# A hybrid decoder layer on one core: norm rows by a store and a broadcast load, and eleven norms' sums by VectorE's 32x32 transposes

## The chip, the cores and the metric

The kernel runs on one core of a Trainium2 chip, as one launch. The metric is the device time of the execution in microseconds, the median of three runs. A core has five engines with a queue each: TensorE (PE, with its weight loads as PEld), VectorE (DVE), ScalarE (ACT), GpSimd (POOL) and SyncE (SP, which here only issues DMAs).

## The reference

One decoder layer on a residual stream of 1024 tokens by 1024 features, float32. Four blocks follow one another; each norms its input, computes, norms its output, and adds it to the stream:

```python
def rmsnorm(x, g):
    y = x32 * lax.rsqrt(jnp.mean(x32 * x32, axis=-1, keepdims=True) + EPS)
    return y * g

h = x
h = h + 0.5 * rmsnorm(swiglu(rmsnorm(h, ffn1_pre_g), ...), ffn1_post_g)
h = h + rmsnorm(hybrid_mixer(rmsnorm(h, mix_pre_g), ...), mix_post_g)
h = h + rmsnorm(memory_cross_attention(rmsnorm(h, xa_pre_g), rmsnorm(mem, mem_g), ...), xa_post_g)
h = h + 0.5 * rmsnorm(swiglu(rmsnorm(h, ffn2_pre_g), ...), ffn2_post_g)
```

The mixer has stick-breaking attention (its output normed with `attn_norm_g`) beside a Mamba-2 SSD scan (its output gated and normed in two groups of 512 features with `ssd_norm_g`), and one output projection for both. So there are some twenty norms for 1024 tokens each, and one for the 256 memory tokens.

## The kernel before, in words

Activations stand with features on the 128 partitions and tokens along the free axis, in two halves (`hh` 0 and 1) of H = 512 tokens and KT = 8 tiles of 128 features: `F[hh][d]` is a block's output, `h[hh][d]` the stream in DRAM, `XH`/`XL` the next block's input as a high and a low part. A float32 matmul is made of three products of such parts (`mm3`), each 128x128 by 128x512.

A norm needs, for each token, a sum of squares over all features, so over the partitions. ScalarE squares the tiles and VectorE adds them into one tile of 128x512 (`sumsq`, line 361). `rms_cols` then multiplies each block of 128 tokens as the stationary operand with a column of 1/1024 (or 1/512): four products of one column give the mean squares of 512 tokens as a column `c` (128 tokens on the partitions, four blocks), followed by a root on ScalarE (L341) and a reciprocal on VectorE (L342). To scale tiles whose tokens lie along the free axis, `rms_rows` turns the column into a row on all 128 partitions: it multiplies each block of `c`, broadcast to 128 columns, with the identity, and ScalarE copies the result from PSUM into `r` (L355). Both use the PSUM tile `ms`, of which there is one; attention's and the scan's transposes use it too.

`post` is the norm of a block's output with the sum into the stream and the norm for the next block: `cols` and `rows` for `r` (`rpost`), `apply` scales and adds (L407, L411), `low` makes the low part (L423), `presum` sums squares for the next norm, whose column and row are `c2` (`cpre`) and `r2_` (`rpre`). `pre` is the same for a norm alone. Where a projection's result leaves PSUM it is multiplied with `rpre` (`evac`), or with `rn` in the mixer's output projection (`norm_row`, `mix_sum`). The columns alone are used as scales in the scores of both attentions.

The order on TensorE is written out: each matmul is tied behind the one before it. `self.clock` adds up modelled TensorE time in ns; a function on `self.later` runs when the clock passes its time, so that its matmuls stand at that place, and `pinned(t)` puts a group there without tying what follows in the program. A planner orders the other queues by its own estimates and by what each instruction waits for; `kp` keeps an instruction of a `later` function in program order. SP's queue is in order too: a DMA that waits for a buffer or for data holds all behind it. Weights come over SP (`wtile`, L182 and L185; `wstream` loads one tile ahead, three buffers).

At the start of attention, `inproj(0)` projects Q, K and V of the first pair of heads. V is transposed in 32x32 blocks on VectorE, stored (L1727), and loaded back with four DMAs that put the blocks in place (L1731); `vtr` splits it. `kevac` writes K's parts to the tiles `k` with four DMAs for each half (`rows`, L1700).

Of the kernel before, what the change touches and what calls it, by code (L numbers as in the profile page):

```python
# [18 lines left out]
P = 128  # L19
S = 1024  # L20
H = 512
# [4 lines left out]
MIXED = 6  # L26
# [21 lines left out]
class Kern:  # L48
# [272 lines left out]

    def rms_cols(self, groups, c, ones=None, r2=None):


        nc = self.nc
        ps = self.t(self.msp, [P, H], F32, "ms", bufs=1)
        nb = 0
        for g, accs in enumerate(groups):
            w = ones[g] if isinstance(ones, list) else self.ones if ones is None else ones
            for b in range(accs[0].shape[1] // P):  # L330
                for i, acc in enumerate(accs):
                    self.mm(
                        ps[:, nb : nb + 1], acc[:, b * P : (b + 1) * P], w, i == 0, i == len(accs) - 1
                    )
                nb += 1
        if r2 is not None:
            self.kp(nc.vector.tensor_tensor(out=c, in0=ps[:, 0:nb], in1=r2, op=ALU.mult))
            self.kp(nc.vector.tensor_tensor(out=c, in0=c, in1=r2, op=ALU.mult))
            self.kp(nc.scalar.activation(c, c, AF.Sqrt, bias=self.eps))
        else:  # L340
            self.kp(nc.scalar.activation(c, ps[:, 0:nb], AF.Sqrt, bias=self.eps))  # L341
        self.kp(nc.vector.reciprocal(c, c))  # L342
        if r2 is not None:
            self.kp(nc.vector.tensor_tensor(out=c, in0=c, in1=r2, op=ALU.mult))

    def rms_rows(self, c, r, behind=None):
# [38 lines left out]

    def post(self, hh, gname, r2, gnext=None, out=None, step=None, spread=True, pins=(23000, 28000), accs=None, at=None, tail=None, hold=False, late=None):

# [8 lines left out]
        r = self.t(self.fp, [P, H], F32, "rpost", bufs=1)  # L396

        def cols():
            self.rms_cols([accs], c, r2=r2)

        def rows():
            self.rms_rows(c, r)

# [79 lines left out]

    def pre(self, hh, accs, t1, t2):
        c = self.t(self.rp, [P, 4], F32, f"cpre{hh}", bufs=2)
        r = self.t(self.rp, [P, H], F32, f"rpre{hh}", bufs=1)
        with self.pinned(t1):
            self.rms_cols([accs], c)
        with self.pinned(t2):
            self.rms_rows(c[:, :], r)  # L490
        self.R[hh], self.C[hh] = r, c
# [487 lines left out]
    def down1(self, sp, wdn, act_d, xs_d, gpost, gnext):  # L979
# [15 lines left out]
        def finish(m, i):  # L995
            if m == 3:
                self.run_later(float("inf"))
                for d in range(4):
                    at(5000 + 4000 * d, squares, 0, d, "acc0")
                self.resid(0, 3500, 16000)  # L1000
            elif m == 4:
                self.run_later(float("inf"))
                for d in range(4, 8):
                    squares(0, d, "acc0")
                self.XH[0] = [self.t(self.xp, [P, H], F32R, f"xh0{d}") for d in range(KT)]
                self.post(0, gpost, self.C[0], gnext, step=2600, accs=accs[:], tail=(20500, 24000), late=38000)
# [9 lines left out]
        self.XH[1] = [self.t(self.xp, [P, H], F32R, f"xh1{d}") for d in range(KT)]  # L1016
        self.post(1, gpost, self.C[1], gnext, step=2000, accs=accs[:], at=(6500, 9000, 10000), tail=(7500, 10500))

# [231 lines left out]
    def ssd(self, close):  # L1250

        nc, ap = self.nc, self.ap
        with self.tc.tile_pool(name=self.nm("ssa"), bufs=1, reuse_waits="tile") as ep, \
# [271 lines left out]
            def group_norm(gr):  # L1525
                c = self.norm_c[gr] = self.t(self.rp, [P, 8], F32, f"cy{gr}")
                self.rms_cols([[y] for y in yacc], c, ones=self.ones512)

# [19 lines left out]
            def keys(n0, n1):  # L1548

                mh, ml, acc, rm = env["mem"]  # L1550
                if n0 == 0:
                    self.mem_c = self.t(self.rp, [P, 2], F32, "cmem")
                    self.rms_cols([[acc]], self.mem_c)
# [93 lines left out]
    def attention(self):  # L1647
        nc, ap = self.nc, self.ap
        with self.pools("at", ["o", "a"], ["w"]) as (op, sp, wsp, pp):
# [52 lines left out]
            def inproj(p):  # L1702
# [12 lines left out]
                def steps(hh, t, before):  # L1715
# [13 lines left out]
                    rows = o.rearrange("(c e) (j q d) -> q e j c d", c=4, q=4, d=32)  # L1729
                    for q in range(4):  # L1730
                        nc.sync.dma_start(  # L1731
                            out=v[32 * q : 32 * q + 32, :].rearrange("e (j c d) -> e j c d", j=4, c=4), in_=rows[q]
                        )
                    return v

# [43 lines left out]
                for n in range(6):  # L1779
# [25 lines left out]
            def mix_row(i):  # L1805
                self.mix_r.append(self.t(self.rp, [P, H], F32, f"rpre{i}", bufs=1))
                return self.rms_rows(self.norm_c[i][:, 0:4], self.mix_r[i], tr_tile)

# [108 lines left out]
            def memory_values(mh, ml):  # L1917

                rm = self.t(self.tp, [P, H], F32, "sq1")[:, 0:MEM]
                self.rms_rows(self.mem_c[:, :], rm)  # L1920
                yield
# [30 lines left out]
            def beside():  # L1952
                late.append(mix_row(1))
                self.first = self.mix_first(ready.pop())
                for n in range(4 * MIXED):
                    if n < 2:
                        for k in ((5, 6), (7,))[n]:
                            mix_split(k)
                    if n == 2:
                        late.pop()()  # L1960
                    if 4 <= n < 11:
# [8 lines left out]
            wo = [self.wsrc("out", 8 * part + d) for n in range(2) for part in (1, 0) for d in range(8)]  # L1970
            self.Wo, self.mix_r, ready, late = self.wstream(wo[0:MIXED]), [], [], []
            for p in range(7):
# [37 lines left out]
    def mix_out(self):  # L2010
# [3 lines left out]
        with self.pools("mo", ["r", "a"], ["b"]) as (rp, sp, sp2, dnp):  # L2014
# [53 lines left out]
            for n, (hh, part) in enumerate(passes):  # L2068
# [3 lines left out]
                def norms(t):  # L2072
                    c = self.norm_c[2] = self.t(self.rp, [P, 4], F32, "ca", bufs=2)
                    with self.pinned(self.clock + t):
                        self.rms_cols([asum[-1:]], c)
                    R[2] = norm_row(2, 0, t + 4000)
# [32 lines left out]
                if n == 1:  # L2109
                    self.run_later(float("inf"))  # L2110
                    self.post(0, "mix_post_g", None, "xa_pre_g", step=5000, spread=False, accs=ends[0], at=(6000, 11500, 14000), tail=(18000, 0))
                    self.resid(1, 5000, 17000)
                if n == 3:
                    self.flush(0)
                    self.post(1, "mix_post_g", None, "xa_pre_g", step=3000, spread=False, accs=ends[1], at=(6000, 10500, 13000), hold=True)


    def xattn(self):
# [3 lines left out]
        with self.pools("xf", ["a", "b", "w"], []) as (sp, sp2, wsp, pp):  # L2122
# [107 lines left out]
            for s in range(8):  # L2230
# [3 lines left out]
                if s == 4:  # L2234
# [5 lines left out]
                    self.run_later(float("inf"))  # L2240
                    self.post(0, "xa_post_g", None, "ffn2_pre_g", step=5000, at=(8500, 16000, 19000))
                if s == 3:
# [46 lines left out]
    def run(self):  # L2289
        nc, tc, ap = self.nc, self.tc, self.ap  # L2290
        with tc.tile_pool(name="const", bufs=1) as cp, tc.tile_pool(name="state", bufs=1, reuse_waits="tile") as xp, \
# [5 lines left out]
            self.place(tp, 64)  # L2297
            self.place(cp, 448)
            self.params = self.t(cp, [P, NPAR], F32, "params")
# [16 lines left out]
            def consts():  # L2316
                cst = self.t(self.fp, [P, 2, P], F32, "rpost")
                nc.sync.dma_start(out=cst, in_=ap["consts"])
                nc.scalar.copy(self.ident, cst[:, 0, :])
                nc.scalar.copy(self.tri, cst[:, 1, :])  # L2320
                for g in (self.par(n, 0, 8) for n in ("ffn1_post_g", "ffn2_post_g")):
# [152 lines left out]
```

## Time and profile before

| | us |
|---|---|
| median of 3 runs (2585.55 to 2587.47) | 2585.72 |
| the profiled execution | 2583.27 |
| its span, first to last instruction | 2581.5 |
| TensorE busy with matmuls | 2564.0 (99%) |
| TensorE's weight loads | 2141.0 (83%) |
| VectorE busy | 2000.7 (78%) |
| ScalarE busy | 1289.0 (50%) |
| GpSimd busy | 576.5 (22%) |

Matmuls overlap in their pipeline, so durations of single ones (some 390 ns for 512 columns) add up to more than the span; what one occupies is the distance from its start to the start of the next. In rows of a timeline the first number is the start, the second the time until the end of the group; "L139" is the line of `mm`, through which nearly every matmul goes, "L142" that of a transpose; "ms<-small,acc" reads: into tile `ms`, from the tiles `small` (the column of ones) and `acc`. "x8" is the number of records; a float32 product has two. A wait in square brackets is the engine's idle time before the instruction, and who ended it. "SPq" is SP's issue of a DMA.

### The profile page before, as it was taken

To read this page: it belongs to the slowest core of one execution; us is meant where nothing else is said; L and a number is where in the kernel's file an instruction comes from. 1 tells how busy PE (TensorE), PEld (TensorE's weight loads), DVE (VectorE), ACT (ScalarE), POOL (GpSimd) and SP (SyncE) were. 2 spreads that over 40 slices of the span, in tenths; PEclk is the share of its full clock that TensorE was granted. 3 is DMA by queue.
4 is the path that set the end of the run, shared out by engine and by line. 5 is a ranking of instruction groups with operands and counts; after the bars stand their busy time and mean duration, and the time that the engine had idled before them with its cause. 6 is when DMAs were issued, how large, how long until landed. Compare 5 with 4: busy or idle time off the path is not lost. (4 is left out here: it accounts for less than half of the span.)

```text
span 2581.5 us, 36855 instructions
## 1 busy us (share of the span) xinstructions
PE 2564.0 (99%) x12786; PEld 2141.0 (83%) x12786; DVE 2000.7 (78%) x3074; ACT 1289.0 (50%) x2302; POOL 576.5 (22%) x674
## 2 busy tenths in 40 slices
PE   9999999999999999999999999999999999999999
PEld 7888888888787778888888898888888888888887
DVE  7988997779689884787787876876656887777777
ACT  7434444555356663555555654455554433334453
POOL 2555553001000001111111110111012655541000
PEclk9999999999999999999999999999999999999999
DMA  6458988655665516666666655547658443327654
GB/s 240 163 180 293 308 290 305 220 185 166 232 205 197 184 72 212 186 177 160 176 171 152 206 167 202 197 155 260 202 185 304 150 162 111 110 82 237 192 175 147
DMA packets 251628, 498.24 MB, mean 193 GB/s; under 512 B 60592, under 2 KB 69168, under 8 KB 251440
## 3 DMA queue, kind: packets, MB, share of 16 engines
q1 hardware_dynamic: 204176, 387.31, 46.4%
q0 software_dynamic: 23360, 65.03, 8.6%
q10 hardware_dynamic: 23904, 43.53, 4.6%
q8 instruction: 101, 1.65, 0.3%
q14 instruction: 87, 0.71, 0.1%
HBM read 331.65 MB, written 143.13 MB: 184 GB/s over the span
## 5 line engine op out<-in xcount | busy, mean ns | idle before, releaser
L139 PE MATMUL mm<-xh,whi 128*128 128x512 f32 x1312 | 516.7, 403 | 1.1 <-DVE ft L668 0.5
L139 PE MATMUL mm<-xh,wlo 128*128 128x512 f32 x1280 | 491.7, 392 | 0.0
L139 PE MATMUL mm<-xl,whi 128*128 128x512 f32 (+1 forms) x1248 | 485.7, 389 | 0.3 <-DVE xl L277 0.3
L139 PEld LDWEIGHTS mm<-xh,wlo 128*128 128x128 f32 x1280 | 240.6, 188 | 52.4 <-DVE wlo L270 0.5
L139 PEld LDWEIGHTS mm<-xh,whi 128*128 128x128 f32 x1312 | 247.0, 188 | 43.1 <-issue 3.9
L139 PEld LDWEIGHTS mm<-xl,whi 128*128 128x128 f32 x1248 | 235.6, 189 | 33.4 <-DVE xl L277 0.8
L1829 DVE TENSOR_TENSOR_SCAN nb<-nb,begin 128x128 f32<-128x128 f32 (+7 forms) x128 | 172.1, 1347 | 32.3 <-ACT nb L1825 31.9
L1825 ACT ACTIVATE nb<-z,scale 128x128 f32<-128x128 f32 (+2 forms) x192 | 109.5, 580 | 89.5 <-PE z L139 88.6
L270 DVE TENSOR_TENSOR wlo<-wraw,whi 128x1024 fp32r<-128x1024 f32 x61 | 74.6, 1223 | 51.3 <-ACT whi L268 50.9
L268 ACT CAST whi<-wraw 128x1024 fp32r<-128x1024 f32 (+1 forms) x77 | 73.9, 959 | 70.4 <-PE mm L139 43.5
L1846 POOL DMA_DIRECT2D mix<-sq x64 | 53.0, 828 | 248.7 <-DVE sq L1844 181.5
L669 ACT ACTIVATE ft<-ft 128x512 f32<-128x512 f32 x88 | 55.5, 632 | 95.5 <-DVE ft L668 94.9
L139 PE MATMUL dn<-xh,wlo 128*128 128x512 f32 x296 | 101.2, 390 | 0.0
L772 POOL TENSOR_TENSOR wc<-raw,wraw 128x512 f32<-128x512 f32 x55 | 80.7, 1467 | 56.4 <-DVE wlo L270 23.4
L268 ACT CAST ath<-tr 128x512 fp32r<-128x512 f32 (+1 forms) x106 | 57.3, 540 | 66.9 <-PE tr L142 61.9
L772 POOL TENSOR_TENSOR wc<-wraw,raw 128x512 f32<-128x512 f32 x56 | 78.9, 1409 | 52.5 <-DVE whi L270 16.5
L871 POOL TENSOR_TENSOR ft<-ft,e 128x512 f32<-128x512 f32 x37 | 59.7, 1614 | 126.3 <-DVE e L867 51.1
L270 DVE TENSOR_TENSOR atl<-tr,ath 128x512 fp32r<-128x512 f32 (+1 forms) x106 | 66.1, 625 | 28.0 <-ACT ath L268 26.9
L139 PE MATMUL mm<-ath,v 128*128 128x256 f32 x320 | 87.8, 297 | 0.0
L139 PE MATMUL dn<-xh,blk 128*128 128x512 f32 x264 | 85.2, 389 | 0.0
L268 ACT CAST wlo<-wc 128x512 fp32r<-128x512 f32 x79 | 49.1, 621 | 69.2 <-PE dn L139 25.4
L139 PE MATMUL mm<-atl,v 128*128 128x256 f32 x320 | 83.1, 282 | 0.0
(601 smaller groups left out, 6795.2 us busy)
## 6 DMA issues: line engine op xcount, KB each, us to landing
whi<-dwhi SPq DMA_DIRECT2D x82, 512.0 KB, 4.1
wlo<-dwlo SPq DMA_DIRECT2D x82, 512.0 KB, 5.4
wraw<-in_w_gu SPq DMA_DIRECT2D x43, 512.0 KB, 4.0
dwhi<-bh SPq DMA_DIRECT2D x78, 256.0 KB, 4.2
dwlo<-bl SPq DMA_DIRECT2D x78, 256.0 KB, 4.2
raw<-in_w_gu SPq DMA_DIRECT2D x37, 512.0 KB, 4.1
wraw<-xs SPq DMA_DIRECT2D x56, 256.0 KB, 2.9
xs<-ft ACTq DMA_DIRECT2D x54, 256.0 KB, 3.0
```

The lines of the kernel that those rows point to most:

```text
L139: self._pe(self.nc.tensor.matmul(out, lhsT, rhs, start=start, stop=stop, skip_group_check=self.more), cost)
L268: self.kp(self.nc.scalar.copy(hi, src))
L270: self.nc.vector.tensor_tensor(out=lo, in0=src, in1=hi.bitcast(F32), op=ALU.subtract)
L669: nc.scalar.activation(t, t, AF.Silu)
L772: inst = (nc.vector if early else nc.gpsimd).tensor_tensor(out=t, in0=a, in1=b, op=op)
L871: nc.gpsimd.tensor_tensor(out=t1, in0=t1, in1=e, op=ALU.mult)
L1825: nc.scalar.activation(nb[:, s0:s1], z[:, 0:n], AF.Sigmoid, scale=sc[:, i : i + 1])
L1829: nc.vector.tensor_tensor_scan(out=nb[:, 0:Wd][:, ::-1], data0=nb[:, 0:Wd][:, ::-1], data1=begin[:, S - Wd : S][:, ::-1], initial=0.0, op0 ...
L1846: nc.gpsimd.dma_start(out=self.mix_d[p][a * 64 : a * 64 + 64, csl], in_=o, accum_op=ALU.add)
```

## The change

`rms_cols` keeps the column in DRAM as well: it stores `c`, in pieces of four bytes, as rows of 128 tokens (`kept`). `row` loads such rows, broadcast over the 128 partitions, into `r`; it takes the place of `rms_rows` in `post` (except the second half after FFN1, `pe=True`), in the norms of the mixer's output projection, in the memory's norm, and in attention for the gated group norms. The input's norms and the last one before FFN2 (`pre`) stay on TensorE.

`turned` takes the place of `rms_cols` for eleven sets of 512 tokens: both gated group norms (two sets each), the next-block norms of both halves after FFN1, the mixer's output norms of both halves, the next-block norm of the mixer's first half, and both norms of the first half after cross-attention. VectorE transposes the tile of squares in 32x32 blocks in place and sums runs of 32; that leaves, for each token, four partial sums in the four quarters of the partitions. One product with `quads`, four 32x32 identities one above the other, adds the quarters: 32 partitions by 16 columns. Root, reciprocal and a store of four-byte pieces follow; where the column is needed too, it is loaded back from there.

Beside that, in `inproj(0)` the loads of the second half of V are issued behind K's, and `vtr(1, ...)` follows; the gated norm's row for the first pass is loaded at step 8 rather than made at steps 10 and 12; and the second half's `apply` in the mixer starts at 14000 rather than 13000.

```diff
-    def rms_cols(self, groups, c, ones=None, r2=None):
+    def rms_cols(self, groups, c, ones=None, r2=None, keep=True):
 ...
+        if keep:
+            kept = self.tc.dram_tile([nb, P], F32, name=self.nm("norm"))
+            nc.sync.dma_start(out=kept.rearrange("b p -> p b"), in_=c)
+            return kept
+
+    def turned(self, accs, ms, wait=0, c=None):
+        nc = self.nc
+        kept = self.tc.dram_tile([4 * len(accs), P], F32, name=self.nm("norm"))
+        ps = self.t(self.msp, [P, H], F32, "ms", bufs=1)
+        parts = []
+        for acc in accs:
+            self.turns = 1 - self.turns
+            parts.append(self.part[self.turns])
+            self.kp(nc.vector.transpose(acc, acc))
+            self.kp(nc.vector.tensor_reduce(out=parts[-1][0], in_=acc.rearrange("p (j k) -> p j k", k=32), op=ALU.add, ...))
+        with self.pinned(self.clock + wait):
+            for n, (part, _) in enumerate(parts):
+                self.mm(ps[0:32, 16 * n : 16 * n + 16], self.quads, part, True, True)
+        for n, (_, x) in enumerate(parts):
+            self.kp(nc.scalar.activation(x, ps[0:32, 16 * n : 16 * n + 16], AF.Sqrt, bias=self.eps[0:32], scale=ms))
+            self.kp(nc.vector.reciprocal(x, x))
+            nc.sync.dma_start(out=kept[4 * n : 4 * n + 4].rearrange("b (q i) -> i (b q)", i=32), in_=x)
+        if c is not None:
+            nc.sync.dma_start(out=c, in_=kept.rearrange("b p -> p b"))
+        return kept
+
+    def row(self, kept, r):
+        self.nc.sync.dma_start(out=r, in_=kept.rearrange("b p -> (b p)").partition_broadcast(P))
 ...
         def cols():
-            self.rms_cols([accs], c, r2=r2)
+            if turn[0]:
+                kept.append(self.turned(accs, 1.0 / D_MODEL, 2000))
+            else:
+                kept.append(self.rms_cols([accs], c, r2=r2, keep=not pe))
         def rows():
-            self.rms_rows(c, r)
+            if pe:
+                self.rms_rows(c, r)
+            else:
+                self.row(kept[0], r)
 ...
-            self.held = [lambda: self.rms_cols([accs2], c2)]
+            self.held = [lambda: kept.append(self.turned(accs2, 1.0 / D_MODEL, 2000, c2) if turn[1]
+                                             else self.rms_cols([accs2], c2, keep=spread))]
 ...
-                q.append((t + t2, lambda: self.rms_rows(c2[:, :], r2_)))
+                q.append((t + t2, lambda: self.row(kept[1], r2_)))
 ...
             def group_norm(gr):
-                self.rms_cols([[y] for y in yacc], c, ones=self.ones512)
+                self.norm_c[gr] = self.turned(yacc, 1.0 / 512.0, 3000)
 ...
-                        self.rms_rows(self.mem_c[:, :], rm)
+                        self.row(self.mem_c, rm)
 ...
-                    for q in range(4):
-                        nc.sync.dma_start(...)
-                    return v
+                    def back():
+                        for q in range(4):
+                            nc.sync.dma_start(...)
+                        return v
+                    return back if hh and p == 0 else back()
 ...
-                vtr(1, tv[1])
+                if p:
+                    vtr(1, tv[1])
                 kevac(evac((yield from last), 1), h1)
+                if p == 0:
+                    vtr(1, tv[1]())
 ...
-                if n == 10:
-                    late.append(mix_row(0))
-                if n == 12:
-                    late.pop()()
+                if n == 8:
+                    mix_row(0)
 ...
             def norm_row(i, hh, at):
-                with self.pinned(self.clock + at):
-                    self.rms_rows(self.norm_c[i][:, 4 * hh : 4 * hh + 4], r)
+                if i < 2:
+                    self.row(self.norm_c[i][4 * hh : 4 * hh + 4], r)
+                else:
+                    with self.pinned(self.clock + at):
+                        self.row(self.norm_c[i], r)
 ...
-  self.post(1, "mix_post_g", ..., at=(6000, 10500, 13000), hold=True)
+  self.post(1, "mix_post_g", ..., at=(6000, 10500, 14000), hold=True, turn=(True, False))
```

More of the change, by code (lines that the diff above doesn't have):

```diff
@@ L384, in resid, with post @@
         self.later += [(self.clock + start + step * d, lambda d=d: one(d)) for d in range(KT)]
-    def post(self, hh, gname, r2, gnext=None, out=None, step=None, spread=True, pins=(23000, 28000), accs=None, at=None, tail=None, hold=False, late=None):
+    def post(self, hh, gname, r2, gnext=None, out=None, step=None, spread=True, pins=(23000, 28000), accs=None, at=None, tail=None, hold=False, late=None, pe=False, turn=(False, False)):
         nc = self.nc
@@ L470, in post @@
             t1, t2 = tail or (t1 + 4000, t2 + 4000)
-            self.held = [lambda: self.rms_cols([accs2], c2)]
+            self.held = [
+                lambda: kept.append(
+                    self.turned(accs2, 1.0 / D_MODEL, 2000, c2) if turn[1] else self.rms_cols([accs2], c2, keep=spread)
+                )
+            ]
             if not hold:
@@ L482, in flush, with pre @@
         self.R[hh], self.C[hh] = self.next_norm
-    def pre(self, hh, accs, t1, t2):
+    def pre(self, hh, accs, t1, t2, pe=True):
         c = self.t(self.rp, [P, 4], F32, f"cpre{hh}", bufs=2)
@@ L487, in pre @@
         with self.pinned(t1):
-            self.rms_cols([accs], c)
+            kept = self.rms_cols([accs], c, keep=not pe)
         with self.pinned(t2):
-            self.rms_rows(c[:, :], r)
+            if pe:
+                self.rms_rows(c[:, :], r)
+            else:
+                self.row(kept, r)
         self.R[hh], self.C[hh] = r, c
@@ L1005, in finish @@
                 self.XH[0] = [self.t(self.xp, [P, H], F32R, f"xh0{d}") for d in range(KT)]
-                self.post(0, gpost, self.C[0], gnext, step=2600, accs=accs[:], tail=(20500, 24000), late=38000)
+                self.post(0, gpost, self.C[0], gnext, step=2600, accs=accs[:], tail=(20500, 24000), late=38000, turn=(False, True))
             elif m == 5:
@@ L1551, in keys @@
                 if n0 == 0:
-                    self.mem_c = self.t(self.rp, [P, 2], F32, "cmem")
-                    self.rms_cols([[acc]], self.mem_c)
+                    self.mem_c = self.rms_cols([[acc]], self.t(self.rp, [P, 2], F32, "cmem"))
                     yield
@@ L1806, in mix_row @@
                 self.mix_r.append(self.t(self.rp, [P, H], F32, f"rpre{i}", bufs=1))
[L1807 removed]
+                self.row(self.norm_c[i][0:4], self.mix_r[i])
             def scores(p, a, c):
@@ L1919, in memory_values @@
                 rm = self.t(self.tp, [P, H], F32, "sq1")[:, 0:MEM]
-                self.rms_rows(self.mem_c[:, :], rm)
+                self.row(self.mem_c, rm)
                 yield
@@ L2110, in mix_out @@
                     self.run_later(float("inf"))
-                    self.post(0, "mix_post_g", None, "xa_pre_g", step=5000, spread=False, accs=ends[0], at=(6000, 11500, 14000), tail=(18000, 0))
+                    self.post(0, "mix_post_g", None, "xa_pre_g", step=5000, spread=False, accs=ends[0], at=(6000, 11500, 14000), tail=(18000, 0), turn=(True, True))
                     self.resid(1, 5000, 17000)
@@ L2114, in mix_out @@
                     self.flush(0)
-                    self.post(1, "mix_post_g", None, "xa_pre_g", step=3000, spread=False, accs=ends[1], at=(6000, 10500, 13000), hold=True)
+                    self.post(1, "mix_post_g", None, "xa_pre_g", step=3000, spread=False, accs=ends[1], at=(6000, 10500, 14000), hold=True, turn=(True, False))
     def xattn(self):
@@ L2240, in xattn @@
                     self.run_later(float("inf"))
-                    self.post(0, "xa_post_g", None, "ffn2_pre_g", step=5000, at=(8500, 16000, 19000))
+                    self.post(0, "xa_post_g", None, "ffn2_pre_g", step=5000, at=(8500, 16000, 19000), turn=(True, True))
                 if s == 3:
@@ L2297, in run @@
             self.place(tp, 64)
-            self.place(cp, 448)
+            self.place(rp, 64)
+            self.place(cp, 64)
+            self.quads, self.turns = self.t(cp, [P, 32], F32, "quads"), 0
+            self.part = [[self.t(cp, [P, 16], F32, f"part{n}"), self.t(cp, [P, 16], F32, f"root{n}")[0:32]] for n in range(2)]
             self.params = self.t(cp, [P, NPAR], F32, "params")
```

29 lines of the change are left out of this document (18 added, 11 removed).

## The prediction

> **What bounds the kernel now.** I read the page's totals first, then TensorE's waits, then the timeline around the norms.
>
> ```profile
> span 2581.5 us, 36855 instructions
> PE 2564.0 (99%) x12786; PEld 2141.0 (83%) x12786; DVE 2000.7 (78%) x3074; ACT 1289.0 (50%) x2302; POOL 576.5 (22%) x674
> PE   9999999999999999999999999999999999999999
> ```
> ```profile
> PE z L139 <- DMA k<-xl: 1.9, 1, 1.9
> PE ms L139 <- DVE atl L270: 1.9, 1, 1.9
> PE dn L139 <- ACT F L1116: 1.3, 1, 1.3
> ```
>
> TensorE is idle for 2581.5 - 2564.0 = 17.5 us of the span, in no slice much, and its longest waits are two of 1.9 us. So the matmul queue, whose order the kernel writes out, sets the time: an instruction taken out of it pulls everything behind it forward by its slot, as long as nothing else becomes late. Those 17.5 us are nearly all that the rest can win.
>
> **What the removed products cost.** The timeline of TensorE around the last cross-attention norm shows one call of each kind inside the stream.
>
> ```profile
> 1930.36 1.05 PE L139 MATMUL ms<-ident,cpost 128*128 128x128 f32 x8
> 1931.17 0.48 PE L139 MATMUL mm<-xl,whi 128*128 128x512 f32 x1
> ...
> 1956.46 0.95 PE L139 MATMUL ms<-small,acc 128*128 128x1 f32 x8
> 1957.27 0.48 PE L139 MATMUL mm<-xl,whi 128*128 128x512 f32 x1
> ```
> ```profile
> 936.40 1.95 PE L139 MATMUL ms<-small,yacc 128*128 128x1 f32 x16
> 938.21 0.48 PE L139 MATMUL mm<-xh,whi 128*128 128x512 f32 x1
> ```
>
> The first number is the start, and the next matmul's start gives the slot. Four float32 products (eight records, two to a product) take 1931.17 - 1930.36 = 0.81 us as a row (`rms_rows`) and 0.81 as a sum (`rms_cols`), although the sum moves a single column; the gated group norm's two sets take 1.81.
>
> Rows: the diff keeps four calls of `rms_rows` on TensorE (the two of the input, `pe=True` in the second half after FFN1, and `pre` before FFN2). It removes fourteen of four blocks (five `rpost`, three `rpre` of the next norm, four of the gated group norms, two of the attention norm) and two of two blocks for the memory: 14 x 0.81 + 2 x 0.40 = 12.1 us.
>
> Sums: seven calls of `turned` with one set and two with two sets stand for eleven sets: 7 x 0.81 + 2 x 1.81 = 9.3 us.
>
> Added on TensorE: eleven products with a stationary of 32 columns and 16 moving ones. None exists; nearest are the small transposes of dt.
>
> ```profile
> 713.18 0.68 PE L142 MATMUL ms<-ident,zs 32*128 32x32 f32 x8
> 713.79 0.50 PE L139 MATMUL mm<-xh,whi 128*128 128x512 f32 x1
> ```
>
> Eight take 0.61 us, 0.076 a record: 0.15 us for two records is the low end, 0.81 / 4 = 0.20 the high one for a float32 product. Alone between big matmuls it may also break their overlap, so I take 0.2, nearer to the rows of the same type: 11 x 0.2 = 2.2 us (1.7 to 4). Net on the queue: 12.1 + 9.3 - 2.2 = 19.2 us less.
>
> **The two long waits.** The first is at the start of attention, where the change also defers the reload of V (`back`) behind K's four copies.
>
> ```profile
> 1032.02 0.50 SPq L1700 DMA_DIRECT2D k<-xl  x1
> 1032.62 2.63 SPq L1731 DMA_DIRECT2D dv<-vt  x4
> 1035.35 1.86 SPq L1700 DMA_DIRECT2D k<-xl  x3
> ```
> ```profile
> 1037.90 0.36 PE L139 MATMUL z<-k,q 128*128 128x256 f32 x1 [1.93 <-DMA k<-xl]
> ```
> ```profile
> 1038.20:1041.50 3.30, 3.30 (x11) 2.75 (x10) 2.35 (x3) 1.34 (x3) 0.00 (x0) 0.50 0.86 226
> 1500.20:1503.60 3.40, 3.40 (x28) 3.40 (x29) 1.64 (x2) 1.13 (x3) 0.00 (x0) 1.00 0.17 45
> ```
>
> The scores of the first head need K's first two copies. The second is issued at 1035.35, behind four V copies that hold SP for 2.6 us, and TensorE resumes 2.55 us after that issue. Moved up it goes at about 1032.6 and lands about 1035.2, before TensorE stops (1037.90 - 1.93 = 1035.97): 1.9 us. V's last copy is issued some 2 us later, and V's second half is first needed in the values of the third block pair, further on. Behind the stall the granted clock is 0.50 for 3.4 us (the third number from the right: 0.50, and 1.00 in the other row); half of it, 1.7 us, is lost, and goes too: together 3.6 us (0 to 3.6). [...]
>
> The second wait is `rms_rows` for the memory's values, which needs the single bank `ms`; the row then no longer uses it. The weight's low half behind it is ready barely earlier, so I take 1.2 us of the 1.9.
>
> **What becomes later.** A norm's row now goes from the reciprocal through a store and a load, both on SP, and the load waits on SP for the store.
>
> ```profile
> raw<-xs SPq DMA_DIRECT2D x54, 256.0 KB, 3.0
> ...
> dv<-vt SPq DMA_DIRECT2D x64, 64.0 KB, 2.6
> ```
> ```profile
> SPq L182 <- PE mm L139: 243.4, 53, 15.1
> ...
> SPq L1731 <- DMA vt<-dv: 32.3, 15, 3.9
> ```
> ```profile
> L1725 DVE STREAM_TRANSPOSE dv<-dv x16: 683/711/714, 1021.2 to 1436.2; 128x512 f32<-128x512 f32 x16
> ```
> ```profile
> L2165 DVE TENSOR_REDUCE st<-dn x32: 407/419/426, 1706.1 to 1881.7; 128x1 f32<-128x256 f32 x32
> ```
>
> The store of 512 four-byte pieces has no row; V's copies, also 512 pieces each, land after 2.6 us. The broadcast row has the size of `raw<-xs`, 3.0. So a row is there about 5.6 us after the reciprocal. In most places the kernel leaves that: the row was a product 3.5 to 7.5 us of schedule behind the sum, the roots of the gated group norms are stored some 450 us ahead, and three to four PSUM banks at 5.4 us a projection cover a late row. VectorE gets 11 x (0.71 + about 0.7 for 512 elements) = 15.5 us, out of its 581 idle; ScalarE loses the copies. `turned` pins its product 2 to 3 us later, which covers those 1.4 to 2.8 us. I cost this at nothing but for two tight places.
>
> ```profile
> 1927.11 0.18 DVE L342 RECIPROCAL cpost<-cpost 128x4 f32<-128x4 f32 x1 [1.83 <-ACT cpost L341]
> ...
> 1932.07 0.75 DVE L407 SCALAR_TENSOR_TENSOR F<-F,params,rpost 128x512 f32<-128x512 f32 x1 [1.73 <-ACT rpost L355]
> ...
> 1953.50 2.28 DVE L369 TENSOR_TENSOR acc<-acc,sq 128x512 f32<-128x512 f32 x3
> ```
> ```profile
> 1929.42 0.32 SPq L182 DMA_DIRECT2D whi<-dwhi  x1
> ```
>
> Second half after cross-attention: VectorE works from the row (1932.07) to the last square sum (1955.78) nearly without a gap, and TensorE's sums stand at 1956.46, 0.7 us later. The row by DMA comes at 1927.29 + 5.6 = 1932.9, 0.9 late: next to nothing if the store goes out before the weight load of 1929.42, about 4 us if behind it. I take 1 us (0 to 5).
>
> ```profile
> 971.01 0.17 DVE L342 RECIPROCAL cmem<-cmem 128x2 f32<-128x2 f32 x1 [0.18 <-ACT cmem L341]
> ...
> 973.99 0.42 DVE L1561 TENSOR_TENSOR dg<-mm,Ct 128x256 f32<-128x256 f32 x1
> ```
>
> The memory's keys: the row is wanted at 973.99 and comes at 971.18 + 5.6 = 976.8; VectorE holds the scan's last chunk behind it for up to 2.8 us. I take 1 us, and 0.5 us for the rest: 2.5 us (0 to 12).
>
> **The sum.** 19.2 + 3.6 + 1.2 - 2.5 = 21.5 us. The profiled execution took 2583.27 us (1.8 beside its span), 2.45 below the median of 2585.72; 2583.27 - 21.5 = 2561.8, and against the median 2564.2 us.
>
> **Rivals.**
> (a) Late rows eat half. Four places (these two, and the posts of the mixer's two halves) each hold TensorE for 3 us: 12 us in place of 2.5, 2574 us. For: SP often sits on a weight load, up to 15.1 us (`L182`), and a store that the planner puts behind it shares that wait. Against: those loads wait because TensorE is not ready for them.
> (b) Slower. The store's round trip stops SP, and weights behind it come late. SP waited in just this way for V's store 15 times, 32.3 / 15 = 2.15 us each. With some 16 such waits passed on in full: 16 x 2.15 = 34 us against 24.0 gained, 2596 us; from 1.5 us passed on for each it decides. Against: of the 15 in attention TensorE's waits show none but the one above. [...]
> (c) No change: the matmul queue isn't the bound, and freed slots turn into waits for weights or operands, about 2585 us. For it speaks that weight loads are busy for 83% only; against it, that 99% of the span has a matmul in flight and the waits listed above are short. [...]
>
> **How the numbers follow.** My forecast 0.66, (a) 0.2, (b) 0.08, (c) 0.06. A measurement tells about 0.2%, 5 us, from no change. Forecast and (a) both end faster: 0.86; same 0.06; slower 0.08. The likeliest case runs from 2558 (both waits gone, nothing late, cheap products) to 2571 (7 us more in the tight places); the range reaches on through (a), 2557 to 2578.
>
> **What will show it.** `ms<-ident` rows of `cpost`, `cy`, `ca`, `cmem` gone but for eight of `cpost`, eleven small products in their place at about 0.2 us, no wait for `k<-xl` and no 0.50 clock at the start of attention, no wait for `atl` near 1480; TensorE's busy time some 17 us less. Wrong, if TensorE waits for `acc` at the second FFN2 norm or for weights behind a norm's store by more than 10 us in all, or if its idle time grows as its busy time falls.

## The result, and the profile after

| | before | after |
|---|---|---|
| median of 5 runs | 2585.55 us | 2655.36 us (2654.38 to 2656.3) |
| ratio after to before | | 1.0272 (95% interval 1.0257 to 1.0287) |
| span of the profiled execution | 2581.5 us | 2653.6 us |
| TensorE idle in it | 17.5 us | 2653.6 - 2576.7 = 76.9 us |
| mean granted clock | 0.999 | 0.985 |

The change makes the kernel 70 us slower, where 21.5 us less was forecast. (One of the ten runs of e4, an experiment below, took 5562.6 us, for a reason not known, and is left out of its ratio.) The totals of the page after, with the busy row of TensorE and its clock:

```profile
span 2653.6 us, 36531 instructions
...
PE 2576.7 (97%) x12600; PEld 2135.7 (80%) x12600; DVE 2016.1 (76%) x3099; ACT 1283.0 (48%) x2289; POOL 576.9 (22%) x674
...
PE   9999999998899998999999999899998999999999
...
PEclk9999999999999999999999999999998999999999
```

TensorE's row has 8s in five slices: two at the end of FFN1, one at the end of the scan, one in the mixer's output projection, and one at the norms after cross-attention. Those are places of the new norms. 186 records fewer run on TensorE, and yet its busy time has grown by 12.7 us. The record of the granted clock says why: 13 stretches at 0.50 inside the span, 75.1 us together, against one of 3.4 us before. Matmuls of 512 columns start every 0.43 us inside such a stretch and every 0.23 us behind it, so work in it takes nearly twice its time. TensorE was busy for 58.0 us of the 75.1, and about half of that was lost, 27 us more than before as an estimate. The balance of the spans, 72 us more: some 59 us more idle and some 27 us of halved clock, less what the products gone from the queue save (19.2 us were forecast; 14 would close the balance).

What TensorE waited for, after (engine, tile and line, what it waited for; us in total, times, longest):

```profile
PE dn L139 <- DVE sq L2057: 9.2, 2, 5.2
PE mm L139 <- DMA wlo<-dwlo: 8.2, 3, 4.1
PE ms L139 <- DVE cpost L344: 7.5, 1, 7.5
PE mm L139 <- DVE dg L1608: 6.5, 1, 6.5
PE dn L139 <- ACT pt L268: 5.5, 2, 5.2
PE dn L139 <- DVE ft L1129: 5.3, 1, 5.3
```

The two waits of before, for `k<-xl` and for `atl`, are gone. In their place stand thirteen of 2 to 7.5 us, and eight of them name VectorE. What VectorE in turn waited for:

```profile
DVE F L449 <- DMA rpost<-norm: 26.9, 4, 13.5
DVE scale L1715 <- DMA cpre<-norm: 22.4, 2, 11.5
...
DVE cb L1107 <- DMA raw<-in_w_dn: 17.9, 12, 7.7
```

VectorE stands for the rows (`rpost`) and for a column (`cpre`), and what comes behind a waiting instruction stands too. The column is needed only by the small `scale` for attention, which starts at 680.48 after 10.92 us idle; `cpost<-ms,cpre` (L337) reads the other half's column, and TensorE's products for it started at 672.00 and took 0.95 us, yet it starts behind `scale`, at 681.82. In the third row VectorE stands for ordinary weights that came late. The transfers (KB each, median us from issue to landing):

```profile
rpost<-norm SPq DMA_DIRECT2D x5, 256.0 KB, 4.8
...
norm<-root SPq DMA_DIRECT2D x11, 2.0 KB, 7.0
...
cpre<-norm SPq DMA_DIRECT2D x4, 2.0 KB, 3.8
norm<-cpost SPq DMA_DIRECT2D x2, 2.0 KB, 10.0
norm<-ca SPq DMA_DIRECT2D x2, 2.0 KB, 10.1
```

A store of 2 KB in four-byte pieces lands after 7.0 us (from 32 partitions) or 10.0 us (from 128), and the row's load another 4.8 later: 12 to 15 us from reciprocal to row, where 5.6 was forecast. One place from end to end, FFN1's first half: SyncE's issues, then VectorE, then TensorE (start, us, ..., in brackets the idle time before and its cause).

```profile
605.68 0.37 SPq L347 DMA_DIRECT2D norm<-cpost  x1
...
606.91 0.33 SPq L1093 DMA_DIRECT2D raw<-in_w_dn  x1
...
614.75 0.32 SPq L378 DMA_DIRECT2D rpost<-norm  x1
```
```profile
617.29 0.69 DVE L1107 TENSOR_TENSOR cb<-xl,raw 128x512 f32<-128x512 f32 x1 [7.68 <-DMA raw<-in_w_dn]
617.90 0.69 DVE L270 TENSOR_TENSOR dx<-cb,dx 128x512 fp32r<-128x512 f32 x1
619.55 1.42 DVE L449 SCALAR_TENSOR_TENSOR F<-F,params,rpost 128x512 f32<-128x512 f32 x2 [0.97 <-DMA rpost<-norm]
```
```profile
623.09 0.84 PE L139 MATMUL dn<-hl,whi 128*128 128x512 f32 x3
629.24 1.62 PE L139 MATMUL dn<-hl,wlo 128*128 128x512 f32 x3 [5.31 <-DVE ft L1129]
```

The weights issued at 606.9, after the store, reach VectorE at 617.29; the row's load cannot go before 614.75; VectorE has lost 8.7 us by 619.55, and TensorE stops for 5.31. How much the DMA engines moved around the same moment, in four kernels (busy time of the engines, granted clock, DMA share, GB/s): after, before, the kernel before with idle stores (607.3 to 613.8 there, `e1_dead_stores` below), and the version without four-byte stores (`e4_all_128`).

```profile
608.00:614.50 6.50, 6.50 (x31) 5.37 (x30) 1.52 (x3) 2.56 (x5) 0.00 (x0) 1.00 0.15 34
```
```profile
608.00:614.50 6.50, 6.50 (x30) 5.38 (x29) 6.50 (x11) 4.68 (x9) 1.08 (x2) 1.00 0.52 170
```
```profile
607.30:613.80 6.50, 6.50 (x31) 5.35 (x30) 6.33 (x11) 4.68 (x9) 1.08 (x2) 1.00 0.23 36
```
```profile
608.00:614.50 6.50, 6.50 (x30) 5.38 (x29) 4.98 (x9) 2.43 (x5) 0.00 (x0) 1.00 0.84 276
```

34 GB/s against 170 and 276. In the changed kernel SyncE also stands and issues little (nothing from 607.71 to 614.75); in the third row it doesn't, and the rate is 36 all the same. So the store is late itself, and while it is under way the other transfers of the core nearly stop.

### The profile page after: what moved, and what is told of

The parts are those of the page before. It is cut to its first block, busy times and chain, and to the rows that moved or that the text cites. A ratio compares the mean times of both kernels' runs of the same rounds, so it can differ in the third digit from the quotient of the medians.

```text
span 2653.6 us, 36531 instructions
## 1 busy us (share of the span) xinstructions
PE 2576.7 (97%) x12600; PEld 2135.7 (80%) x12600; DVE 2016.1 (76%) x3099; ACT 1283.0 (48%) x2289; POOL 576.9 (22%) x674
## 3 DMA queue, kind: packets, MB, share of 16 engines
q1 hardware_dynamic: 216784, 391.29, 47.3%
## 5 line engine op out<-in xcount | busy, mean ns | idle before, releaser
L139 PE MATMUL dn<-xh,whi 128*128 128x512 f32 x240 | 82.7, 389 | 0.0
```

Source lines behind the costliest of these rows:

```text
L139: self._pe(self.nc.tensor.matmul(out, lhsT, rhs, start=start, stop=stop, skip_group_check=self.more), cost)
```

## The experiments

Theory A: stores in pieces of four bytes land late and hold up the other transfers; rows and columns come too late for VectorE, where what follows stands behind them, and the stops of TensorE that follow are lengthened by the halved clock. Theory B: only the lateness costs. Theory C (the prediction's rival b): SyncE stands for the round trip, and the weights queued behind it come late. Theory D: any round trip over DRAM is too long for where the consumers stand. Each ratio is against runs of the kernel before on the same chip (their medians were 2583.9, 2584.7 and 2584.1 us).

| run | what | us | ratio (95%) |
|---|---|---|---|
| e1 | before + 16 idle stores, 4-byte pieces | 2607.5 | 1.0087 (1.0068 to 1.0107) |
| e12 | before + 16 idle stores, 128-byte pieces | 2584.1 | 1.0001 (0.9992 to 1.0011) |
| e3 | after, 11 of 16 stores in 128-byte pieces | 2624.4 | 1.0154 (1.0132 to 1.0176) |
| e4 | after, all 16 in 128-byte pieces | 2583.2 | 0.9992 (0.9982 to 1.0002) |
| e6 | e4 + three more hops in DRAM | 2632.4 | 1.0182 (1.0168 to 1.0195) |
| e7 | after, loads issued by GpSimd | 2665.6 | 1.0308 (1.0293 to 1.0323) |
| e8 | e4, FFN1's norms on TensorE | 2577.9 | 0.9966 (0.9954 to 0.9979) |
| e10 | e8, cross-attention's too | 2572.8 | 0.9960 (0.9947 to 0.9972) |
| e11 | e10, the mixer's output norms too | 2574.2 | 0.9964 (0.9951 to 0.9976) |
| e9 | before + V's loads deferred | 2583.9 | 1.0000 (0.9991 to 1.0009) |

**Idle stores (e1), and their control (e12).**

```diff
+        if dead:
+            for b in range(0, nb, 4):
 ...
+                kept = self.tc.dram_tile([w, P], F32, name=self.nm("norm"))
+                nc.sync.dma_start(out=kept.rearrange("b p -> p b"), in_=c[:, b : b + w])
```
and in e12
```diff
+                nc.sync.dma_start(out=kept.rearrange("b (q i) -> (b q) i", i=32), in_=groups[b // 4][0][0 : 4 * w, 0:32])
```

> The kernel before with the sixteen sets of norm columns (the same places as in the changed kernel) also stored in four-byte pieces, and nobody reads them: no row and no column comes later than before, and nothing waits on SyncE's queue. Theory A (a store of 512 four-byte pieces holds up the other transfers for 7 to 8 us while it lands): weights come late at some of the sixteen places, 5 to 20 us slower, 2590 to 2606 us, and the time between issue and landing of weight loads beside a store grows to 7 us or more. Theory B (only the lateness of the rows and columns costs, through the engines that wait for them): 2585.5 us, within 3. Theory C (SyncE's queue stands behind loads that wait for the store): also 2585.5, since no load waits.

> The control for the sixteen idle stores: the kernel before, with sixteen idle stores of the same 2 KB at the same norms, in 16 pieces of 128 bytes from the tile of squares. Theory A (the four-byte pieces stop the other transfers): no change, 2584 us within 3, against 2607.5 with pieces of four bytes. If any store and its receipt on SyncE's queue cost as much: 2600 to 2608.

Measured 2607.5 us, just above the range of A, and 2584.1 for the control. Nobody reads these stores. The trace puts one wait down to them, GpSimd's 26.6 us ahead of `k`, which the kernel before has just as long for ScalarE. So what they cost, some 23 us, they cost through the other transfers alone. Loads of weight tiles (`whi`, `wlo`, `raw`, `wraw`) issued within 4 us behind one of these stores landed after 9.5 to 13.2 us (twelve loads), behind one of e12's after 3.1 to 4.7 (thirteen). ScalarE, which splits the weights, then waits for some of them, and in the kernel before it has no such wait (e1):

```profile
ACT whi L268 <- DMA wraw<-in_w_out: 9.6, 4, 4.4
ACT whi L268 <- DMA wraw<-in_w_q: 9.1, 1, 9.1
```

The same bytes at the same norms in pieces of 128 bytes cost nothing, although SyncE stood for the tiles to be stored as long in e12 as in e1 (35 and 34 us in all). B and C, which had e1 at 2585.5, are too small by themselves.

**Layouts (e2, e5).** Idle stores of one size, 2 KB (pf 16 KB), in six shapes; e5 differs from e2 by its source:

```diff
+            nc.sync.dma_start(out=..., in_=(self.ident[:, 0:4], self.ident[:, 0:4], self.ident[0:16, 0:32], ...)[n])   # e2
+            nc.sync.dma_start(out=..., in_=(acc[:, 0:4], acc[:, 0:4], acc[0:16, 0:32], acc[0:4, 0:P], acc[0:32, 0:16], acc[:, 0:32])[n])   # e5
```

> The kernel before with some twenty idle stores of a constant tile at its norms, in turn in six layouts: pa 512 pieces of 4 bytes from 128 partitions (the columns' store), pb 128 pieces of 16 bytes, pc 16 of 128 bytes, pd 4 of 512 bytes, pe 512 of 4 bytes from 32 partitions (the store of the small products' result), pf 128 of 128 bytes. Read are the times from issue to landing. Theory A (the pieces' size decides): pa and pe 7 to 10 us, pc and pd 2 to 3, pb between, pf under 4. If any store to DRAM at these places lands late, whatever its shape, all six are near 7 us; if the number of pieces decides, pb and pf are both near a quarter of pa.

e2 told nothing: a store from a constant waits for nothing, and all seventeen went out in the first 45 us, on top of each other (2601.0 us in one run).

> The six layouts again, in the kernel before, now stored from the tile of squares right behind each norm's sum, so that they stand one by one among the weight loads from FFN1's end on (before, all had been issued in the first 45 us). Theory A (the size of the pieces decides): 512 pieces of 4 bytes (pa, pe) land after 7 to 10 us, 16 of 128 (pc) and 4 of 512 bytes (pd) after about 2, 128 of 16 bytes (pb) and 128 of 128 bytes (pf) tell the size from the number: if the number of pieces under 512 bytes decides, pb and pf take the same time, about 3 to 4 us; if the size, pb is nearer to pa and pf nearer to pc. If a store's place decides, the six overlap.

```profile
pa<-acc SPq DMA_DIRECT2D x2, 2.0 KB, 9.9
pb<-acc SPq DMA_DIRECT2D x2, 2.0 KB, 5.0
...
pc<-acc SPq DMA_DIRECT2D x2, 2.0 KB, 4.6
pe<-acc SPq DMA_DIRECT2D x2, 2.0 KB, 6.9
```

The one run took 2595.3 us. Over all samples: pa 9.6 to 11.9 us, pe 6.3 to 6.9, pb 1.4 and 5.0, pc 2.8 to 4.6; for pd and pf the trace has no landing. The two shapes of 512 pieces keep apart from the others and have the times of the changed kernel. Whether the size of a piece or their number decides stays open: 128 pieces of 16 bytes and 16 of 128 can't be told apart by so few samples.

**Larger pieces (e3, e4).** The result of the small product is turned once more on VectorE, and lies then as 16 rows of 32 tokens; in e4 the five columns as well, in four transfers each:

```diff
 ...
-            nc.sync.dma_start(out=kept[4 * n : 4 * n + 4].rearrange("b (q i) -> i (b q)", i=32), in_=x)
+            self.kp(nc.vector.transpose(accs[n][0:32, 32:64], accs[n][0:32, 0:32]))
+            nc.sync.dma_start(out=kept[4 * n : 4 * n + 4].rearrange("b (q i) -> (b q) i", i=32), in_=accs[n][0:16, 32:64])
 ...
-            nc.sync.dma_start(out=kept.rearrange("b p -> p b"), in_=c)
+            self.kp(nc.vector.transpose(acc[:, 32:64], acc[:, 0:32]))
+            for q in range(4):
+                nc.sync.dma_start(out=kept[:, 32 * q : 32 * q + 32], in_=acc[32 * q : 32 * q + nb, 32:64])
```

> The changed kernel, but the result of the small product (32 by 16) is turned once more by VectorE, and stored in 16 pieces of 128 bytes: eleven of the sixteen scattered stores are gone, five (two posts, the two attention norms, the memory) remain. Theory A: those eleven rows and columns come about 5 us earlier, and the stops behind them go with their halved clock: 2610 to 2630 us. If the round trip through SyncE's queue is what costs, whatever the pieces (theory C): 2645 to 2656. If only places with a scattered store of 128 partitions matter: no change, 2655.

> As the run before, and the other five stores too go in pieces of 128 bytes (the column is turned in 32x32 blocks by VectorE and stored by four transfers of four pieces), so that no scattered store is left; loads, places and order as in the changed kernel. Theory A: rows come some 6 to 7 us after the reciprocal, as the prediction had them: 2565 to 2595 us, TensorE idle for 20 to 35 us. Theory C (SyncE stands for the round trip): 2640 or more. Theory D (the consumers stand too early in VectorE's order, and any round trip over DRAM is too long for them): 2600 to 2630, with the same VectorE waits at two thirds of their length.

Both came out in A's range, 2624.4 and 2583.2 us. In e3 the two kinds stand side by side:

```profile
norm<-acc SPq DMA_DIRECT2D x7, 2.0 KB, 1.7
...
norm<-yacc SPq DMA_DIRECT2D x4, 2.0 KB, 2.3
norm<-cpost SPq DMA_DIRECT2D x2, 2.0 KB, 10.0
```

1.7 us against 10.0 for the same 2 KB. The whole loss of 70 us hung on the shape of sixteen stores of 2 KB: with their shape alone changed (and the turns that this takes), e4 is level with the kernel before. The loads of the columns (`cpre<-norm`) are still in four-byte pieces there; in e3 they land after 3.5 us.

**Lateness without four-byte stores (e6).**

```diff
+    def relay(self, kept):
+        for _ in range(3):
+            old, kept = kept, self.tc.dram_tile(list(kept.shape), F32, name=self.nm("relay"))
+            self.nc.sync.dma_start(out=kept, in_=old)
+        return kept
```

> The version without any scattered store, but each norm goes through three further tiles in DRAM (copies of 2 KB in pieces of 512 bytes) before its row and column are loaded: rows come about 6 us later again, SyncE stands as long as in the changed kernel, and no four-byte piece is written. If the lateness of rows and columns (with SyncE's standing) is most of the loss: 2620 to 2640 us, as 72 us less the 23 that the idle stores cost by themselves would have it. If what costs is the stop of the other transfers alone: 2583 to 2595.

2632.4 us, 49 more than e4, with no four-byte store. The row after FFN1's first half was issued 12.4 us behind its store (e4 3.8, the changed kernel 9.1). So lateness costs even without the stop of the other transfers; SyncE's longer standing is part of it here, and e6 doesn't part the two. As these rows are some 3 us later than the changed kernel's, how its own 70 us split between the two isn't read from this.

**SyncE's standing (e7).**

```diff
-            nc.sync.dma_start(out=c, in_=kept.rearrange("b p -> p b"))
+            nc.gpsimd.dma_start(out=c, in_=kept.rearrange("b p -> p b"))
-        self.nc.sync.dma_start(out=r, in_=kept.rearrange("b p -> (b p)").partition_broadcast(P))
+        self.nc.gpsimd.dma_start(out=r, in_=kept.rearrange("b p -> (b p)").partition_broadcast(P))
```

> The changed kernel with its scattered stores as they are on SyncE, but the loads of rows and columns issued by GpSimd: SyncE no longer stands for the store's round trip, GpSimd does. Theory C (weights behind a standing SyncE are what comes late): most of the 72 us is won back, under 2610 us. Theory A (rows late, transfers stopped): 2640 to 2660, no change of more than 15 us, as the rows come no earlier.

2665.6 us: with SyncE free nothing is won, and 10 us are lost. C as the main cause is out. (GpSimd stands in SyncE's place now, and issues the stream's loads and stores, so the 10 us need not be a price of SyncE's.)

**Where a row over DRAM pays (e8, e10, e11).** Sites of e4 are put back to `rms_cols` and `rms_rows` (`pe2` does it for the next block's norm):

```diff
-  self.post(0, gpost, ..., late=38000, turn=(False, True))
+  self.post(0, gpost, ..., late=38000, pe=True, pe2=True)          # e8, FFN1; second half alike
-  self.post(0, "xa_post_g", ..., turn=(True, True))
+  self.post(0, "xa_post_g", ..., pe=True, pe2=True)                # e10; second half pe=True
-  self.post(0, "mix_post_g", ..., tail=(18000, 0), turn=(True, True))
+  self.post(0, "mix_post_g", ..., tail=(18000, 0), pe=True)        # e11; second half alike, at 13000
```

> The version without scattered stores, with FFN1's norms (both posts and both next norms) as in the kernel before, on TensorE. There TensorE waited for 5.9 us and ran 10 us at half clock. It gets back three rows and two sums, 3.7 us, and loses the waits and the slow stretch: 2583.2 - 7.3 = 2576 us (2570 to 2581). If these waits come from elsewhere, 2583 to 2588.

> The version with FFN1's norms on TensorE and no scattered store, with the norms after cross-attention on TensorE too. By the matmuls' starts that version was 12.8 us ahead of the kernel before at the end of cross-attention's scores and 10.1 us ahead behind its norms, although 3.7 us of products had gone there. If rows over DRAM cost more there than they save: 2575 us, 2 to 3 less than the 2577.9 of that version. If what was lost there has other causes, 3 to 4 us more, 2581.

> The version of the run before with the mixer's output norms on TensorE too: by DMA go only the gated group norms, the attention norm's rows and the memory's rows, all with slack. Three sums and two rows more on TensorE: 3 x 0.65 + 2 x 0.81 = 3.6 us more than the run before, if those norms had cost nothing else there; equal or faster, if their rows were late too.

Measured 2577.9, 2572.8 and 2574.2 us. At the end of FFN1 e4 falls from 1.7 us ahead of the kernel before to 5.4 behind (at 640 and 700 us). About 5 of these 7 us come near 646 us, where TensorE waits twice for 0.9 us, for weight parts from ScalarE, and then runs at half clock for 6.8 us (mean clock 0.998 in e4's profiled execution, 1.000 in e8's); with FFN1's norms on TensorE (e8) they are gone, but how the rows bring them about is not traced. The rest is D's mechanism at one place:

```profile
665.37 0.33 SPq L377 DMA_DIRECT2D norm<-acc  x1
...
667.40 0.38 SPq L379 DMA_DIRECT2D cpre<-norm  x1
667.83 0.49 SPq L384 DMA_DIRECT2D rpre<-norm  x1
```
```profile
671.44 0.17 DVE L1721 TENSOR_SCALAR scale<-cpre 128x4 f32<-128x4 f32 x1 [6.10 <-DMA cpre<-norm]
```

The store is there after 2.0 us, and yet VectorE stands for 6.10 us, since `scale` needs the column to come back over DRAM. After cross-attention e8 loses 2.9 us against the kernel before (the last two rows of the table below), although products of 3.7 us are gone from there; e10, with them back, loses 0.2. By the medians e10 is 5 us below e8, where 2 to 3 were expected, but their intervals overlap: that a row over DRAM costs more there than it saves is likely, not shown. For the mixer's output norms the runs say nothing: e11 was expected 3.6 us above e10 and came 1.4 above, inside both intervals. e10 beats both kernels: 0.40% less than before (0.28 to 0.53). It keeps by DMA the rows of the gated group norms, of the attention norm, of the memory and of the mixer's two output norms, and `turned` for five sums (seven sets).

How far each kernel is behind the kernel before at the same large matmul, by the starts of the profiled executions (us; minus is ahead):

| at (us of before) | after | e1 | e6 | e4 | e8 | e10 |
|---|---|---|---|---|---|---|
| 600, FFN1 near its end | -0.1 | -0.8 | 0.9 | -0.8 | -0.4 | 0.9 |
| 780, in the scan | 22.5 | 5.1 | 20.3 | 5.4 | 0.3 | 1.0 |
| 1072, attention | 32.8 | 10.7 | 26.5 | 1.7 | -3.7 | -2.9 |
| 1549, output projection begins | 29.8 | 10.6 | 23.2 | -1.5 | -6.9 | -6.1 |
| 1740, cross-attention's scores | 50.6 | 23.4 | 41.0 | -7.0 | -11.9 | -10.8 |
| 2048, FFN2 | 72.4 | 26.7 | 47.3 | -4.5 | -9.0 | -10.6 |

In the changed kernel each stretch with norms adds 10 to 23 us; only attention, where rows have slack, gives 3.0 back, and in the versions without four-byte stores 3.2 or 3.3. The two rows and the memory's last one that are gone there are worth 2 x 0.81 + 0.40 = 2.0 us, so some 1.0 to 1.3 is left for the wait for `atl` (1.2 was forecast).

**V's loads deferred, alone (e9).**

```diff
-                vtr(1, tv[1])
+                if p:
+                    vtr(1, tv[1])
                 kevac(evac((yield from last), 1), h1)
+                if p == 0:
+                    vtr(1, tv[1]())
```

> The kernel before with one part of the change alone: the loads of V's second half behind K's copies at the start of attention, every norm as it was. The prediction's step: the wait of 1.9 us for K and 1.7 us of halved clock go, 3.6 us less, about 2580.5 us (2579 to 2583). If a new wait takes their place, 2584 to 2587.

2583.9 us, no change: within 2.3 us either way. K's wait is gone. But SyncE's order behind V's four copies is another too: the low half of a later weight, issued at 1042.22 in the kernel before, goes out at 1053.47, behind Q's copies, and TensorE waits for it (SyncE's issues, then TensorE):

```profile
1031.38 2.52 SPq L1700 DMA_DIRECT2D k<-xl  x4
1034.01 3.81 SPq L1733 DMA_DIRECT2D dv<-vt  x4
...
1053.47 0.46 SPq L182 DMA_DIRECT2D wlo<-dwlo  x1
```
```profile
1059.40 0.50 PE L139 MATMUL mm<-xh,wlo 128*128 128x512 f32 x1 [0.88 <-DMA wlo<-dwlo]
```

## Why the prediction was wrong

- **The bound and the removed products: right.** The matmul queue sets the time. The rows are gone, a small product's slot is 0.16 us (0.2 taken), and where rows have slack the queue moves forward by what the slots add up to: e10 keeps eight of the fourteen rows, the memory's two and seven of the eleven sets (8 x 0.81 + 2 x 0.40 + 2 x 1.81 + 3 x 0.81 - 7 x 0.16 = 12.2 us), and measured 11.3 by the medians (7 to 14). The match is rougher than it looks, as the two long waits are gone as well and 5 of the 24.0 us forecast were theirs.
- **The store: the step that failed.** "The store of 512 four-byte pieces has no row; V's copies, also 512 pieces each, land after 2.6 us." The row was chosen by the number of pieces, and it is a load from DRAM in pieces of 128 bytes. The store took 7.0 to 10.0 us, and e4 shows that this alone decided between 2655 and 2583 us. No upper end was set for this price, though it stood in sixteen places; at three times 2.6 a row would have come 10.8 us behind the reciprocal, where the prediction found 3.5 to 7.5 us of schedule.
- **What such a store does to others: no term at all.** Some 23 us by e1, through loads, of weights among others, that nobody had tied to the norm.
- **"In most places the kernel leaves that. I cost this at nothing but for two tight places."** Wrong even with the store at 2 us: e4 stands at 2583, 19 us above the forecast. At FFN1's end a reloaded column came late, and e8 wins 5 us by going back to TensorE there; e10 wins as much again by the medians after cross-attention, which is not clear of noise. That the column of `turned` makes a second trip (`cpre<-norm`), with VectorE's `scale` waiting for it, was not counted.
- **The halved clock: counted on one side only.** The prediction took 1.7 us of it as a gain at the start of attention, and none as a price of new waits, where it came to some 27 us.
- **The two long waits: right that they go; the first oversized in time.** 3.6 us for it was the end of a bound that began at 0. e9 shows no gain in the medians: a new wait of 0.88 us, for a weight that moved behind Q's copies, takes part of it back, and in e12 the same wait for K (2.1 us) was followed by no halved clock, so that this half of the 3.6 us isn't there in every run. The queue was looked at for K and V, not for the weights behind them. The second wait's 1.2 us agree with the 1.0 to 1.3 of the table.
- **Rivals.** (a), late rows, had the kind of thing right, with four places of 3 us. (b) had the right side but another mechanism: SyncE's standing, which e7 clears. (c) is out: after e10's products left the queue, the time fell by about their slots. The line on what would make the prediction wrong, idle time that grows as busy time falls, is what happened to the idle time (17.5 to 76.9 us); busy time grew too, by the halved clock. Of the likeliest case, 2558 to 2571, the lower end fits only a count from the profiled execution (2583.27), while the rest is counted from the median; nothing hangs on it.

## What to carry to other kernels

A store's price went by the shape of what it writes (medians for 2 KB: 7.0 to 10.1 us in four-byte pieces in the changed kernel, 1.6 to 3.1 in pieces of 128 bytes in e3 and e12): look for its row among stores with pieces of that size, and where there is none, set a wide upper end and multiply it by the number of places. A turn in 32x32 blocks on VectorE (0.2 us) ahead of a small store makes its pieces 128 bytes and took 70 us out of this kernel. A trip over DRAM pays where its reader stands far behind it (e10: 0.40% less than before). Here it takes some 7 to 9 us as an estimate (2.0 to 3.8 until the store has landed in e4, 4.8 for the row in the changed kernel); at the end of FFN1, where VectorE reads within that time, four products, 0.81 us together, were cheaper (e8).

## What the runs showed of the hardware

- 2 KB stored to DRAM in 512 pieces of four bytes: landing after 7.0 us from 32 partitions (the changed kernel's median) and after 7.2 to 11.9 from 128 (e1's single stores; medians of 8.1 to 10.6 by tile). In 16 pieces of 128 bytes: medians of 1.6 to 3.1 (e3, e12), with one of e12's at 7.0. A load of 512 four-byte pieces (`cpre<-norm`): 3.5 to 4.1 (e3, after, e7). While the four-byte store is under way, what the DMA engines move falls from some 170 to 34 GB/s, about 6.5 us long (at 608 us); why, no run here shows.
- The changed kernel's thirteen stretches of halved clock lasted 3.4 us (five), 6.8 (seven) and 10.2 (one). In the stop of 5.31 us that began at 623.9 the clock halved at 627.0, for 6.8 us (after; PE busy first, the clock third from the right):

```profile
623.50:626.90 3.40, 0.43 (x2) 0.01 (x1) 3.40 (x7) 3.17 (x6) 0.65 (x2) 1.00 0.61 188
627.00:633.80 6.80, 4.56 (x11) 3.63 (x12) 6.80 (x12) 1.86 (x3) 0.54 (x1) 0.50 0.53 183
634.00:637.40 3.40, 3.40 (x17) 2.81 (x16) 3.40 (x6) 2.22 (x4) 0.54 (x1) 1.00 0.63 189
```

Two waits of 2.0 us were each followed by one stretch of 3.4 us in the changed kernel, and one of 1.4 us in e1; one of 2.1 us in e12 was followed by none (mean clock 1.000 in its profiled execution). What decides between them, no run here shows.
